# Hybrid decoder block: engines in program order from the first unit on, attention prepared in short steps

## Chip, cores and metric

One core of a Trainium2 chip runs the kernel. The time is device microseconds from launch to the end, the median of several runs. The engines that matter are TensorE (PE), VectorE (DVE), ScalarE (ACT), GpSimd (POOL) and SyncE (SP), which issues the DMAs of the weights.

## What is computed

512 tokens of width 1024 go through one layer: one input projection, two causal mixers (a spatial gating unit and gated linear attention), a gated sum, an output projection, and a feed-forward block, each of the last two followed by a LayerNorm.

```python
p   = x @ W_in + b_in    # u | v | q | k | v_gla | r | a_low | g_A | g_B
y_a = gelu(u) * (W_s @ layer_norm(gelu(v)) + b_s)          # 128-position chunks, 8 groups, causal
log_f = log_sigmoid(a_low @ w_gate2 + b_gate) / 16         # per key channel
# gated linear attention, 4 heads: cum = cumsum(log_f) within a chunk
scores[t, s] = sum_d q[t, d] * k[s, d] * exp(cum[t, d] - cum[s, d])   # s <= t
o   = scores @ v + (q * exp(cum)) @ state
state = exp(total) * state + (k * exp(total - cum)).T @ v
y_b = rms_norm(o) * gla_norm_g * silu(r)
m   = sigmoid(g_A) * y_a + sigmoid(g_B) * y_b
h   = layer_norm(alpha * x + m @ W_out)
out = layer_norm(alpha * h + relu(h @ W_1)**2 @ W_2)
```

## The kernel before

Every fp32 product is made of three fp32r products: an operand is split into a high part (`xh`, `wh`) and the rest (`xl`, `wl`), and `passes` (L194) yields high x high, high x low, low x high. Weights come in chunks of 128x1024: SP loads `raw` (three buffers, L114), ScalarE casts it to `wh` (L92), VectorE subtracts for `wl` (L93). Seven chunks of `wh`, `wl` are kept (`W_BUFS`); `split_to(n)` writes the load, the cast and the subtraction of all chunks up to n at the place in the program where it is called.

The matrix work is cut into units of 24 matmuls of 512 columns, each into one of the four `ps_m` PSUM buffers. The units are counted in slots: slots 0 to 7 are V (two column halves by four token tiles, `row_unit`, L197), 8 to 15 U (`col_job`, L605), 16 to 19 queries and keys of the second pair of heads, 20 to 27 the values VG, 28 to 35 the branch gate GA, 36 to 51 r and g_B, 52 to 59 the output projection. The feed-forward block follows, whose second product is made by seven products of quarter blocks (`seven_products`), the sums of these (`together`, L905) and a last stage `f` (L984) with LN 2 behind it, token tile by token tile. Ahead of slot 0 stand a warm-up of PE on ones (`wu`, L241), q and k of the first pair (`first`, L265) and the low-rank gate input (`pa`, L317).

Attention of a pair of heads is prepared between the units: `at(n, f)` puts a step into slot n and `pump`, called behind each unit, runs what is planned there. The steps of a pair are `gates` (log-sigmoid as Abs, Exp, Ln and a running sum `cum`), three levels of block distance (32, 8, 2), each with `level_diff` (differences of `cum` for key factors `kt` and query factors `qt`), `level_prep` (exponentials, times k and q) and `level_score` for two heads (products `sc`, copied under masks into `AT`), two diagonal scores `sd`, `inter` (the factors `QI`, `kd` between chunks), and `kd_turn` (transposes `pt`, L390). `chunk_out` makes a chunk's output and state. The query differences run on POOL, three instructions for a level (L413).

What sets the order: PE runs in program order from the start. Instructions of VectorE, ScalarE and POOL are ordered by the tile scheduler up to L803, where `manual_schedule` for all engines begins; behind it they too stand as written. The pools around the change: `ps_s` has one buffer (`sc`, `sd`), `ps_a` two (`pz`, `pt`, `pm`, `po`), the tag "kt" one buffer that `ab`, `kd`, `kt` and the diagonal's `dr` share, the tag "qt" two.

Of the kernel before, what the change touches and what calls it, by code (L numbers as in the profile page):

```python
# [8 lines left out]
F32 = mybir.dt.float32  # L9
F32R = mybir.dt.float32r  # L10
# [5 lines left out]
P = 128  # L16
# [24 lines left out]
WARM = (128,) * 7 + (64,) * 5  # L41
QT_BUFS = 2
DIFF_K = "vector"
DIFF_Q = "gpsimd"
MUL_K = "vector"
MUL_Q = "vector"
# [3 lines left out]
def hybrid_block(  # L50
# [131 lines left out]
    plan, slot = {}, [0]  # L182

    def at(n, *fs):
        plan.setdefault(n, []).extend(fs)

    def pump():
        for f in plan.pop(slot[0], []):
            f()
        slot[0] += 1  # L190
# [6 lines left out]
    def row_unit(ah, al, consume):  # L197
# [3 lines left out]
        for ti, t in enumerate(range(NT)):  # L201
            ps = ps_m.tile([P, 512], F32, name=f"ps_{u0}_{t}", tag="ps")
            tsl = slice(t * P, (t + 1) * P)
            for k in range(KT):
                split_to(u0 + max(k // 2 + 1, (W_BUFS if ti < NT - 1 else W_BUFS + k // 2)))
# [6 lines left out]
            pump()  # L212
        split_to(u0 + 4 + W_BUFS)
# [26 lines left out]
    for n in WARM:  # L240
        nc.tensor.matmul(wu[:, :n], ones, ones[:, :n], start=True, stop=True)  # L241
# [108 lines left out]
    def gates(pr):  # L350
        hp = pr.hp
        lf = gt.tile([P, 2, T], F32, name=f"lf{hp}", tag="lf")
        cum = gt.tile([P, 2, T], F32, name=f"cum{hp}", tag="cum")
        ab = gt.tile([P, 2, T], F32, name=f"ab{hp}", tag="kt")
        for j in range(2):
            h = 2 * hp + j
            pz = ps_a.tile([P, 512], F32, name=f"pz{h}", tag="aux")
            nc.tensor.matmul(pz, w2s[:, h * DK : (h + 1) * DK], a_sb, start=True, stop=True)
            bg = col("g2", h)
            nc.scalar.activation(ab[:, j, :], pz, AF.Abs, bias=bg)  # L360
            nc.vector.tensor_scalar(lf[:, j, :], pz, bg, 0.0, op0=ALU.add, op1=ALU.min)
        nc.scalar.activation(ab, ab, AF.Exp, scale=-1.0)
        nc.scalar.activation(ab, ab, AF.Ln, bias=1.0)
        nc.vector.tensor_tensor(lf, lf, ab, op=ALU.subtract)
# [6 lines left out]
        pr.lf, pr.cum = lf, cum  # L371

    def inter(pr):

        hp = pr.hp
        nc.scalar.activation(pr.QI, pr.cum, AF.Exp, scale=1.0 / TEMP)
        nc.vector.tensor_mul(pr.QI, pr.QI, pr.q)
        cv = pr.cum.rearrange("p j (c s) -> p (j c) s", s=P)
        tot = cv[:, :, P - 1 : P]
        nc.scalar.activation(pr.et, tot.rearrange("p c o -> p (c o)"), AF.Exp, scale=1.0 / TEMP)  # L380
        kd = gt.tile([P, 2 * NCH, P], F32, name=f"kd{hp}", tag="kt")
        nc.vector.tensor_tensor(kd, tot.broadcast_to([P, 2 * NCH, P]), cv, op=ALU.subtract)
# [13 lines left out]
    def level_diff(pr, lv):  # L396

        hp, h = pr.hp, LEVELS[lv]
        kt = gt.tile([P, 2 * T], F32, name=f"kt{hp}_{lv}", tag="kt")
        qt = gt.tile([P, 2 * NCH, 192], F32, name=f"qt{hp}_{lv}", tag="qt", bufs=QT_BUFS)  # L400
        nb, na = 2 * T // h, 2 * T // (4 * h)
        cb = flat(pr.cum).rearrange("p (b s) -> p b s", s=h)
        getattr(nc, DIFF_K).tensor_tensor(
            kt.rearrange("p (b s) -> p b s", s=h),
            cb[:, :, h - 1 : h].broadcast_to([P, nb, h]),
            cb,
            op=ALU.subtract,
        )
        c4 = flat(pr.cum).rearrange("p (a i s) -> p a i s", i=4, s=h)
        qv = qt.rearrange("p c n -> p (c n)").rearrange("p (a i s) -> p a i s", i=6, s=h)  # L410
# [8 lines left out]
        pr.kt, pr.qt = kt, qt  # L419

    def level_prep(pr, lv):
        h = LEVELS[lv]
        kt, qflat = pr.kt, pr.qt.rearrange("p c n -> p (c n)")
        nc.scalar.activation(kt, kt, AF.Exp, scale=1.0 / TEMP)
        nc.scalar.activation(qflat, qflat, AF.Exp, scale=1.0 / TEMP)
        getattr(nc, MUL_K).tensor_tensor(kt, kt, flat(pr.k), op=ALU.mult)
        q4 = flat(pr.q).rearrange("p (a i s) -> p a i s", i=4, s=h)
        qv = qflat.rearrange("p (a i s) -> p a i s", i=6, s=h)
        for d, s0 in STEPS:
            n = 4 - d  # L430
            getattr(nc, MUL_Q).tensor_tensor(
                qv[:, :, s0 : s0 + n, :], qv[:, :, s0 : s0 + n, :], q4[:, :, d:4, :], op=ALU.mult
            )

    def diag_prep(pr, j):

        hp = pr.hp
        two = gt.tile([P, 1536], F32R, name=f"dt{hp}_{j}", tag="qt", bufs=QT_BUFS)
        raw = gt.tile([P, 768], F32, name=f"dr{hp}_{j}", tag="kt")
        par = lambda a, o: a[:, j, :].rearrange("p (m o) -> p m o", o=2)[:, :, o]  # L440
        nc.vector.tensor_mul(raw[:, 0:512], pr.q[:, j, :], pr.k[:, j, :])
        pair = raw[:, 512:768]
        nc.scalar.activation(pair, par(pr.lf, 1), AF.Exp, scale=1.0 / TEMP)
        nc.vector.tensor_mul(pair, pair, par(pr.q, 1))
        nc.vector.tensor_mul(pair, pair, par(pr.k, 0))
        split(two[:, 0:768], two[:, 768:1536], raw)
        pr.two = two

    def diag_score(pr, j):
        sc = ps_s.tile([P, 1024], F32, name=f"sd{pr.hp}_{j}", tag="sc")  # L450
        for c0, c1 in ((0, 512), (512, 768)):
            for i in range(2):
                nc.tensor.matmul(
                    sc[:, c0:c1], ones_r, pr.two[:, 768 * i + c0 : 768 * i + c1], start=(i == 0), stop=(i == 1)
                )
        at_ = pr.AT[:, j]
        nc.vector.copy_predicated(
            at_,
            masks[:, 3, 64:192].bitcast(U32).unsqueeze(1).broadcast_to([P, NCH, P]),
            sc[:, 0:512].rearrange("p (c s) -> p c s", s=P),  # L460
        )
        nc.vector.copy_predicated(
            at_.rearrange("p c (m o) -> p c m o", o=2)[:, :, :, 1],
# [668 lines left out]
```

## Time and profile before

| | us |
|---|---|
| median of 3 runs (lowest, highest) | 764.57 (763.75, 764.64) |
| profiled execution | 764.65 |
| its span | 762.9 |
| PE busy | 750.0 |
| VectorE, ScalarE, POOL busy | 489.4, 356.3, 68.1 |

The span is what the trace covers; 1.75 us of the profiled execution lie around it. A busy time counts every instant at which an instruction of the engine ran. PE's matmuls overlap their forerunners, so an interval of 100% can still be a slow one, which the granted clock tells. A wait in the trace is the idle time of an engine ahead of an instruction, put down to the instruction that released it.

### The profile page before, as it was taken

The page shows a single profiled execution, that of the slowest core. Times are in us where ns is not written, and L with a number is a line of the kernel's source. Part 1 is how long each engine was busy: PE and PEld are TensorE (multiplying, and loading weights), DVE is VectorE, ACT ScalarE, POOL GpSimd, SP SyncE. Part 2 cuts the span into 40 slices and gives each one's busy share as a digit, 9 for nine tenths or more (in the row PEclk, how much of TensorE's full clock was granted, in tenths as well). Part 3 has the DMA queues.
Part 4 walks back from the last instruction along what each step waited for, and adds up shares of the span by engine and source line. Part 5 has one row for each costly group of instructions (what it writes and reads, how often), then busy time and mean ns, then how long its engine had stood idle before and what let it go on. Part 6 is the DMA issues. An engine that isn't in the chain of part 4 may idle for free.

```text
span 762.9 us, 8863 instructions
## 1 busy us (share of the span) xinstructions
PE 750.0 (98%) x3504; PEld 628.3 (82%) x3504; DVE 489.4 (64%) x587; ACT 356.3 (47%) x457; POOL 68.1 (9%) x86
## 2 busy tenths in 40 slices
PE   9998999999999999999999999999999999999996
PEld 8887888878888888888888988888888888888785
DVE  7369767668766542454548535774678667778975
ACT  7376864354146444444322444554554544445300
POOL 1015400013302212000001000000000000000011
PEclk9999999999999999999999999999999999999999
DMA  8523332110341232323231423444244433434111
GB/s 338 201 97 104 104 131 82 61 53 26 111 138 56 78 129 82 113 90 104 89 125 63 153 83 99 136 148 142 73 148 139 138 109 113 164 112 165 56 56 55
DMA packets 25465, 85.15 MB, mean 112 GB/s; under 512 B 3088, under 2 KB 3344, under 8 KB 25424
## 3 DMA queue, kind: packets, MB, share of 16 engines
q1 hardware_dynamic: 25280, 84.33, 32.7%
q8 instruction: 27, 0.44, 0.2%
q10 hardware_dynamic: 144, 0.26, 0.1%
q14 instruction: 14, 0.11, 0.0%
HBM read 82.48 MB, written 2.10 MB: 111 GB/s over the span
## 4 chain that ended last, share of the span: by engine, by line
PE 88%; DVE 5%; ACT 3%; issue 2%; POOL 1%; DVEq 0%; POOLq 0%
PE f L602 23%; PE m L898 14%; PE ps L208 12%; PE gb L602 6%; PE r L602 6%; PE u L602 6%; PE f L984 5%; PE ga L602 4%; PE first L265 3%; PE qk L602 2%; PE sc L472 2%; DVE wl L93 1%; POOL qt L413 1%; PE po L498 1%; PE po L500 1%
## 5 line engine op out<-in xcount | busy, mean ns | idle before, releaser
L93 DVE TENSOR_TENSOR wl<-raw,wh 128x1024 fp32r<-128x1024 f32 x141 | 175.0, 1251 | 137.2 <-ACT wh L92 130.6
L92 ACT CAST wh<-raw 128x1024 fp32r<-128x1024 f32 x141 | 145.3, 1045 | 122.7 <-PE ps L208 27.5
L602 PE MATMUL f<-xh,wh 128*128 128x512 f32 (+1 forms) x288 | 105.4, 366 | 0.0
L602 PE MATMUL f<-xl,wh 128*128 128x512 f32 (+1 forms) x288 | 105.2, 365 | 0.0
L602 PE MATMUL f<-xh,wl 128*128 128x512 f32 (+1 forms) x288 | 105.2, 365 | 0.0
L898 PE MATMUL m<-wh,oh 128*128 128x512 f32 x168 | 65.4, 389 | 0.0
L898 PE MATMUL m<-wl,oh 128*128 128x512 f32 x168 | 65.4, 389 | 0.0
L898 PE MATMUL m<-wh,ol 128*128 128x512 f32 x168 | 65.4, 389 | 0.0
L602 PEld LDWEIGHTS f<-xh,wl 128*128 128x128 f32 x288 | 54.3, 189 | 8.8
L602 PEld LDWEIGHTS f<-xl,wh 128*128 128x128 f32 x288 | 54.3, 189 | 8.7
L602 PEld LDWEIGHTS f<-xh,wh 128*128 128x128 f32 x288 | 54.3, 189 | 8.6
L208 PE MATMUL ps<-wh,xh 128*128 128x512 f32 x128 | 51.3, 401 | 0.0
L208 PE MATMUL ps<-wl,xh 128*128 128x512 f32 x128 | 50.1, 391 | 0.0
L208 PE MATMUL ps<-wh,xl 128*128 128x512 f32 x128 | 50.1, 391 | 0.0
L827 ACT ACTIVATE F<-f 128x512 f32<-128x512 f32 (+1 forms) x28 | 15.0, 537 | 72.4 <-PE f L602 72.4
L127 DVE TENSOR_TENSOR raw<-raw,raw 128x1024 f32<-128x1024 f32 x30 | 36.7, 1222 | 8.4 <-DMA raw<-in_w_all 8.4
L413 POOL TENSOR_TENSOR qt<-cum 128x768 f32<-128x768 f32 (+2 forms) x18 | 31.4, 1774 | 115.8 <-DVE cum L368 102.9
L898 PEld LDWEIGHTS m<-wl,oh 128*128 128x128 f32 x168 | 31.6, 188 | 6.6
L898 PEld LDWEIGHTS m<-wh,ol 128*128 128x128 f32 x168 | 31.5, 188 | 6.6
L898 PEld LDWEIGHTS m<-wh,oh 128*128 128x128 f32 x168 | 31.5, 188 | 6.5
L993 POOL TENSOR_TENSOR rs_l<-rs_l,nhalf 128x1 f32<-128x1 f32 x4 | 4.0, 988 | 328.6 <-DVE rs_l L992 328.6
L92 ACT CAST oh<-d 128x1024 fp32r<-128x1024 f32 x15 | 15.8, 1050 | 36.4 <-DVE d L824 36.4
(231 smaller groups left out, 1528.5 us busy)
## 6 DMA issues: line engine op xcount, KB each, us to landing
raw<-in_w_all SPq DMA_DIRECT2D x136, 512.0 KB, 3.3
bufB<-in_head SPq DMA_DIRECT2D x4, 512.0 KB, 7.9
xr<-in_x SPq DMA_DIRECT2D x8, 256.0 KB, 3.7
out<-bufA SPq DMA_DIRECT2D x8, 256.0 KB, 2.0
bufA<-in_head SPq DMA_DIRECT2D x3, 512.0 KB, 5.3
brow<-in_b_in SPq DMA_DIRECT2D x4, 256.0 KB, 5.9
g<-in_ln_g SPq DMA_DIRECT2D x2, 512.0 KB, 4.4
b<-in_ln_b SPq DMA_DIRECT2D x2, 512.0 KB, 4.3
```

What stands on the lines that cost most here:

```text
L92: nc.scalar.copy(hi, src)
L93: nc.vector.tensor_tensor(lo, src, hi.bitcast(F32), op=ALU.subtract)
L127: nc.vector.tensor_tensor(raw, raw, other[0], op=ALU.add if STREAM[i][0] == "sum" else ALU.subtract)
L208: nc.tensor.matmul(ps, s_, m_, start=(k == 0 and i == 0), stop=(k == KT - 1 and i == 2))
L265: nc.tensor.matmul(first[e], s_, m_[:, k, :], start=(k == 0 and i == 0), stop=(k == KT - 1 and i == 2))
L413: getattr(nc, DIFF_Q).tensor_tensor(qv[:, :, s0 : s0 + n, :], c4[:, :, d:4, :], c4[:, :, 0:n, h - 1 : h].broadcast_to([P, na, n, h]), op=A ...
L472: nc.tensor.matmul(sc[:, c, 0:192], pr.kt[:, jc * P : (jc + 1) * P], pr.qt[:, jc, :], start=True, stop=True)
L498: nc.tensor.matmul(po, pr.AT[:, j, c, :], vs, start=True, stop=(c == 0))
L602: nc.tensor.matmul(ps, s_, m_, start=(k == 0 and i == 0), stop=(k == KT - 1 and i == 2))
L827: nc.scalar.activation(dst, ps, AF.Relu)
L898: nc.tensor.matmul(ps, s_, m_, start=(k == 0 and i == 0), stop=(k == 3 and i == 2))
L984: nc.tensor.matmul(ps, s_, m_, start=(f == 0 and i == 0), stop=(f == 7 and i == 2))
```

## The change

The `manual_schedule` of VectorE, ScalarE and POOL (PE had it) now begins behind `low_rank`, ahead of the V units, so all four engines run in the written order from slot 0 on. To write that order, the slots get phases: MID in the middle of a `row_unit`, MM behind the unit's matmuls, MAIN, and LATE behind the unit's chunk splits. The attention steps are cut up over these and lie at other slots:

| step | pair 0 before | after | pair 1 before | after |
|---|---|---|---|---|
| gates | 1 | 0 MID, 1 | 18 | 17, 18 |
| level 0: diff, prep, scores | 3, 3, 5, 6 | 4, 5, 6, 7 | 20, 21, 22, 23 | 21, 23, 24, 25 |
| level 1 | 7, 7, 8, 10 | 7, 8, 9, 10 | 23, 24, 25, 26 | 25, 27, 28, 29 |
| level 2 | 11, 11, 12, 13 | 10, 11, 12, 13 | 26, 26, 28, 29 | 29, 30, 31, 32 |
| diagonal scores | 14, 16 | 15, 16 | 31, 32 | 34, 35 |
| inter | 16 | 2, 3 | 32 | 19, 20 |
| kd_turn (both heads) | 17, 18 | 4 | 33, 34 | 21 |
| mixing of 8 groups | 14 to 21 | 10 to 17 | | |
| chunk_out | 29 to 32 | 28, 31, 32, 33 | 35 to 38 | 36 to 39 |

The query factors of block distance 1 are an exponential of one difference; those of distance 2 and 3 are products of it with the factors of whole blocks between (`whole`, copied by ScalarE). VectorE makes that one difference; the exponential covers 768 elements instead of 1536. `gates_a` puts both heads' products `pz` into one `ps_s` tile. The warm-up is nine matmuls of 128 columns instead of seven of 128 and five of 64. `rstd_of` adds on VectorE. `together` works on one token tile: ahead of the last stage only quarter 7 of tile 0 is summed, the other sums stand behind the pieces of tiles 0 and 1, and `bn_stats` ahead of them.

```diff
-WARM = (128,) * 7 + (64,) * 5
+WARM = 9
...
-            nc.gpsimd.tensor_scalar(dst, src, EPS, None, op0=ALU.add)
+            nc.vector.tensor_scalar(dst, src, EPS, None, op0=ALU.add)
...
             for k in range(KT):
+                if k == KT // 2:
+                    pump(MID)
...
-            pump()
-        split_to(u0 + 4 + W_BUFS)
+            pump(MM, MAIN)
+            if ti == NT - 1:
+                split_to(u0 + 4 + W_BUFS)
+            pump(LATE)
...
+    def gates_a(pr):
+        lf = gt.tile([P, 2, T], F32, name=f"lf{pr.hp}", tag="lf")
+        ab = gt.tile([P, 2, T], F32, name=f"ab{pr.hp}", tag="kt")
+        both = ps_s.tile([P, 2, T], F32, name=f"pz{pr.hp}", tag="sc")
+        heads = [(j, 2 * pr.hp + j) for j in range(2)]
+        for j, h in heads:
+            nc.tensor.matmul(both[:, j, :], w2s[:, h * DK : (h + 1) * DK], a_sb, start=True, stop=True)
+        for j, h in heads:
+            nc.scalar.activation(ab[:, j, :], both[:, j, :], AF.Abs, bias=col("g2", h))
+            nc.vector.tensor_scalar(lf[:, j, :], both[:, j, :], col("g2", h), 0.0, op0=ALU.add, op1=ALU.min)
         nc.scalar.activation(ab, ab, AF.Exp, scale=-1.0)
         nc.scalar.activation(ab, ab, AF.Ln, bias=1.0)
...
+    ctx.enter_context(
+        tc.manual_schedule(
+            engines={getattr(mybir.EngineType, e) for e in ("PE", "DVE", "Activation", "Pool")}
+        )
+    )
...
-        for d, s0 in STEPS:
-            n = 4 - d
-            getattr(nc, DIFF_Q).tensor_tensor(
-                qv[:, :, s0 : s0 + n, :],
-                c4[:, :, d:4, :],
-                c4[:, :, 0:n, h - 1 : h].broadcast_to([P, na, n, h]),
-                op=ALU.subtract,
-            )
...
+        nc.vector.tensor_mul(qv[:, :, 0:3, :], qv[:, :, 0:3, :], q4[:, :, 1:4, :])
+        for o, i0, n in ((3, 1, 2), (5, 4, 1)):
+            nc.vector.tensor_mul(
+                qv[:, :, o : o + n, :],
+                qv[:, :, i0 : i0 + n, :],
+                pr.whole[:, :, 0:n].unsqueeze(3).broadcast_to([P, na, n, h]),
             )
...
+        at(between[0], lambda: gates_b(pr))
+        at(between[1], lambda: inter_a(pr))
+        at(between[1], lambda: inter_e(pr), phase=LATE)
+        at(between[2], lambda: inter_b(pr))
+        kd_turn(between[3], pr)
...
+    at(0, lambda: gates_a(pr0), phase=MID)
+    plan_pair(pr0, (1, 2, 3, 4), ((4, 5, 6, 7), (7, 8, 9, 10), (10, 11, 12, 13)), 13)
...
-            together(7, ((1, 4),))
+            together(7, 0, ((1, 4),))
         if ORDER[n] == 1:
-            together(6, ((1, 3),))
-            together(7, ((1, 1),))
+            together(7, 0, ((1, 1),))
...
-    together(7, ((-1, 5),))
-    together(3, ((1, 5),), (0, 1))
+    together(7, 0, ((-1, 5),))
+    later = {
+        (0, 0): [(6, 0, ((1, 3),)), (3, 0, ((1, 5),), (0, 1))],
+        (0, 1): [(7, 1, ((1, 4), (1, 1), (-1, 5))), (6, 1, ((1, 3),)), (3, 1, ((1, 5),), (0, 1))],
+        (1, 0): [(4, t, ((1, 2),), (1, 0)) for t in range(2)],
+        (1, 1): [(6, t, ((1, 1), (-1, 2))) for t in range(2)],
+    }
...
-            if t == 0:
-                together(*(((4, ((1, 2),), (1, 0))), (6, ((1, 1), (-1, 2))))[pi])
             nc.vector.bn_stats(st2[t][:, pi, :], z[:, sl])
+            for part in later.get((t, pi), ()):
+                together(*part)
```

How the change moves instructions is shown at three places. The first is ScalarE in the V stage, from the cast of chunk 10 on (`bufB<-vt0_n` is the gelu of token tile n, `ab0` the gates of pair 0). Before:

```order
L92 CAST wh10_385<-raw10_372 128x1024
L360 ACTIVATE ab0_450<-pz0_451,cols_sb_101 128x512
L581 ACTIVATE bufB_92<-vt0_1_444 128x512
L360 ACTIVATE ab0_450<-pz1_455,cols_sb_101 128x512
L362 ACT_TABLE_LOAD
L362 ACTIVATE ab0_450<-ab0_450 128x1024
L363 ACT_TABLE_LOAD
L363 ACTIVATE ab0_450<-ab0_450 128x1024
L92 CAST wh11_506<-raw11_374 128x1024
```

After, up to the exponential for QI:

```order
L88 CAST wh10_384<-raw10_369 128x1024
L363 ACTIVATE ab0_403<-pz0_404,cols_sb_101 128x512 x2
L365 ACTIVATE ab0_403<-ab0_403 128x1024
L366 ACT_TABLE_LOAD
L366 ACTIVATE ab0_403<-ab0_403 128x1024
L659 ACT_TABLE_LOAD
L659 ACTIVATE bufB_92<-vt0_0_425 128x512
L659 ACTIVATE bufB_92<-vt0_1_453 128x512
L659 ACTIVATE bufB_92<-vt0_2_492 128x512
L391 ACT_TABLE_LOAD
L391 ACTIVATE QI0_313<-cum0_456 128x1024
```

The gates follow the cast of chunk 10 at once, three gelus stand together behind them, and the exponentials between chunks (`QI`, `kd`, `et`) come ahead of the casts of chunks 11 to 13.

The second place is VectorE in the same stretch, from the subtraction that ends the gates (`vt0_n` takes a unit's result, `sgst` are LayerNorm statistics). Before:

```order
L364 TENSOR_TENSOR lf0_448<-lf0_448,ab0_450 128x1024
L579 TENSOR_TENSOR vt0_2_495<-ps_4_2_470,brow_382 128x512
L368 SCALAR_TENSOR_TENSOR cum0_449<-ones_97,lf0_448 128x128 x8
L93 TENSOR_TENSOR wl11_507<-raw11_374,wh11_506 128x1024
L403 TENSOR_TENSOR kt0_0_546<-cum0_449 128x1024
L582 BN_STATS sgst2_380<-bufB_92 128x6
L93 TENSOR_TENSOR wl12_519<-raw12_376,wh12_518 128x1024
L93 TENSOR_TENSOR wl13_531<-raw13_389,wh13_530 128x1024
L579 TENSOR_TENSOR vt0_3_542<-ps_4_3_499,brow_382 128x512
L426 TENSOR_TENSOR kt0_0_546<-kt0_0_546,k0_313 128x1024
```

After:

```order
L372 TENSOR_TENSOR lf0_402<-lf0_402,ab0_403 128x1024
L376 SCALAR_TENSOR_TENSOR cum0_456<-ones_97,lf0_402 128x128 x8
L661 BN_STATS sgst0_377<-bufB_92 128x6
L657 TENSOR_TENSOR vt0_2_492<-ps_4_2_467,brow_381 128x512
L386 TENSOR_TENSOR kd0_495<-cum0_456 128x1024
L661 BN_STATS sgst1_378<-bufB_92 128x6
L89 TENSOR_TENSOR wl11_509<-raw11_371,wh11_508 128x1024
L89 TENSOR_TENSOR wl12_521<-raw12_373,wh12_520 128x1024
L89 TENSOR_TENSOR wl13_533<-raw13_388,wh13_532 128x1024
L657 TENSOR_TENSOR vt0_3_544<-ps_4_3_501,brow_381 128x512
L396 TENSOR_TENSOR QI0_313<-QI0_313,q0_309 128x1024
L397 TENSOR_TENSOR kd0_495<-kd0_495,k0_310 128x1024
```

The chunk subtractions wl11 to wl13 stand between the difference `kd` and the products for QI and `kd`; behind these, at slot 4, PE transposes `kd`. The level's `kt`, `qt` come later.

The third place is VectorE ahead of the last stage, from the last addition of product 1 on (`Fs`, `xl` are operands of that stage, `bufB` and `acc` the sums of quarters). Before:

```order
L875 TENSOR_TENSOR acc1_3168<-acc1_3168,m2_1_1_5250 128x512
L908 TENSOR_TENSOR bufB_92<-bufB_92 128x2x512
L908 TENSOR_TENSOR bufB_92<-bufB_92,acc1_3168 128x2x512
L93 TENSOR_TENSOR Fs_5278<-Flast_4767,Fs_5278 128x512 x4
L93 TENSOR_TENSOR wl142_5315<-raw142_5228,wh142_5314 128x1024
L93 TENSOR_TENSOR xl_90<-Flast_4767,xh_89 128x512 x4
L875 TENSOR_TENSOR acc5_3170<-acc5_3170,m2_5_0_5328 128x512
L93 TENSOR_TENSOR xl_90<-raw143_5261,xh_89 128x1024
L93 TENSOR_TENSOR wl144_5352<-raw144_5273,wh144_5351 128x1024
```

After:

```order
L958 TENSOR_TENSOR acc1_3165<-acc1_3165,m2_1_1_5247 128x512
L992 TENSOR_TENSOR bufB_92<-bufB_92,acc1_3165 128x512
L89 TENSOR_TENSOR Fs_5274<-Flast_4764,Fs_5274 128x512 x4
L89 TENSOR_TENSOR wl142_5311<-raw142_5225,wh142_5310 128x1024
L89 TENSOR_TENSOR xl_90<-Flast_4764,xh_89 128x512 x4
L958 TENSOR_TENSOR acc5_3167<-acc5_3167,m2_5_0_5324 128x512
L89 TENSOR_TENSOR xl_90<-raw143_5258,xh_89 128x1024
L89 TENSOR_TENSOR wl144_5348<-raw144_5270,wh144_5347 128x1024
L89 TENSOR_TENSOR wl145_5358<-raw145_5314,wh145_5357 128x1024
```

One sum of half the width stands ahead of the operands in the place of two; between the subtractions of the operands nothing has moved.

## Rows read from the trace of the kernel before

**Rows 1.** The page: busy time of each engine, share of the span, instructions.
```profile
PE 750.0 (98%) x3504; PEld 628.3 (82%) x3504; DVE 489.4 (64%) x587; ACT 356.3 (47%) x457; POOL 68.1 (9%) x86
```

**Rows 2.** What PE waited for: us in total, times, longest.
```profile
PE sc L472 <- DVE qt L431: 2.1, 1, 2.1
PE pz L358 <- DVE mx L649: 1.3, 1, 1.3
...
PE f L984 <- DVE xl L93: 0.5, 1, 0.5
PE sc L472 <- DVE AT L484: 0.3, 1, 0.3
PE f L984 <- DVE wl L93: 0.3, 2, 0.2
PE po L498 <- ACT bufB L516: 0.3, 1, 0.3
```

**Rows 3.** Chain of waits, 28 to 110 us: start, us, what.
```profile
49.41 1.23 DVE lf L364
...
51.15 2.62 DVE cum L368 x8
...
66.96 2.61 PE sc L472 x8
69.57 6.07 PE ps L208 x24
75.64 1.30 PE sc L472 x8
76.94 5.45 PE ps L208 x24
```

**Rows 4.** Windows: us, busy of five engines (instructions), PEclk, DMA share, GB/s.
```profile
67.30:70.60 3.30, 3.30 (x11) 3.06 (x10) 2.65 (x5) 3.12 (x3) 0.44 (x2) 0.50 0.15 27
158.20:162.00 3.80, 3.80 (x18) 3.17 (x17) 1.60 (x3) 3.56 (x4) 0.00 (x0) 1.00 0.40 142
```

**Rows 5.** Timeline of PE at 157 us: start, us, engine, line, operation, tiles.
```profile
156.06 0.50 PE L358 MATMUL pz<-a_sb,w2s 128*128 128x512 f32 x1
157.85 0.51 PE L358 MATMUL pz<-a_sb,w2s 128*128 128x512 f32 x1 [1.29 <-DVE mx L649]
```

**Rows 6.** Timeline of POOL in the V stage.
```profile
53.85 12.08 POOL L413 TENSOR_TENSOR qt<-cum 128x768 f32<-128x768 f32 x6 [29.40 <-DVE cum L368]
```

**Rows 7.** Timelines of ScalarE and VectorE, V stage; landing times of weight loads there.
```profile
43.95 0.68 ACT L360 ACTIVATE ab<-pz,cols_sb 128x512 f32<-128x512 f32 x1
44.65 1.28 ACT L362 ACT_TABLE_LOAD   x1
...
33.39 2.36 DVE L93 TENSOR_TENSOR wl<-raw,wh 128x1024 fp32r<-128x1024 f32 x2 [0.19 <-ACT wh L92]
...
43.56 0.75 DVE L361 TENSOR_SCALAR lf<-pz,cols_sb 128x512 f32<-128x512 f32 x1 [0.26 <-ACT ab L360]
...
DMA to landing us min/median/max: 3.1/3.3/4.3
```

**Rows 8.** Timeline of all engines at the start.
```profile
1.07 5.14 PE L241 MATMUL wu<-ones 128*128 128x128 f32 x24 [1.07 <-POOL bal L284]
...
4.29 0.62 ACT L255 CAST xh<-bufA 128x512 fp32r<-128x512 f32 x1 [1.58 <-DMA bufA<-in_head]
...
6.02 1.17 PE L265 MATMUL first<-xh,wh 128*128 128x512 f32 x4
```

**Rows 9.** Timelines of VectorE, ScalarE and PE around the final stage's first matmuls.
```profile
705.55 1.22 DVE L908 TENSOR_TENSOR bufB<-bufB,acc 128x1024 f32<-128x1024 f32 x1
...
713.75 1.05 ACT L92 CAST wh<-raw 128x1024 fp32r<-128x1024 f32 x1 [2.58 <-DMA raw<-in_w_all]
...
713.62 0.39 PE L984 MATMUL f<-xh 128*128 128x512 f32 x1
...
717.36 0.39 PE L984 MATMUL f<-wh,Fs 128*128 128x512 f32 x1
```

More of the change, by code (lines that the diff above doesn't have):

```diff
@@ L239, in hybrid_block @@
     wu = ps_a.tile([P, 512], F32, name="wu", tag="aux")
-    for n in WARM:
-        nc.tensor.matmul(wu[:, :n], ones, ones[:, :n], start=True, stop=True)
+    for i in range(WARM):
+        nc.tensor.matmul(wu[:, :P], ones, ones, start=True, stop=True)
     for i in range(4):
@@ L348, in pair_new, with gates_b @@
         return pr
[L350 to L361, printed above, removed]
+    def gates_a(pr):
[8 more added lines that the diff above has]
+            nc.vector.tensor_scalar(lf[:, j, :], both[:, j, :], col("g2", h), 0.0, op0=ALU.add, op1=ALU.min)
         nc.scalar.activation(ab, ab, AF.Exp, scale=-1.0)
         nc.scalar.activation(ab, ab, AF.Ln, bias=1.0)
-        nc.vector.tensor_tensor(lf, lf, ab, op=ALU.subtract)
+        pr.lf, pr.ab = lf, ab
+    def gates_b(pr):
+        lf = pr.lf
+        cum = gt.tile([P, 2, T], F32, name=f"cum{pr.hp}", tag="cum")
+        nc.vector.tensor_tensor(lf, lf, pr.ab, op=ALU.subtract)
         for j in range(2):
@@ L435, in diag_prep @@
[L435 to L447, printed above, removed]
@@ L629, in hybrid_block, with mix_bias, take @@
         row_unit(xh, xl, v_take(half, bias_row(C_V + half * 512)))
-    def mix_bias():
-        for i in range(2):
-            pb = ps_a.tile([P, 4, P], F32, name=f"pb{i}", tag="aux")
-            nc.tensor.matmul(pb, ones, wst[:, 4 * i : 4 * i + 4, :], start=True, stop=True)
+    def mix_bias(n):
+        def take(i, pb):
             for g in range(4 * i, 4 * i + 4):
@@ L659, in hybrid_block, with products, mix, take @@
-    for g in range(KT):
-        at(S_QK - 2 + g, lambda g=g: mix(g))
+        def products():
+            for i in range(2):
+                pb = ps_a.tile([P, 4, P], F32, name=f"pb{i}", tag="aux")
+                nc.tensor.matmul(pb, ones, wst[:, 4 * i : 4 * i + 4, :], start=True, stop=True)
+                at(n, lambda i=i, pb=pb: take(i, pb))
+        at(n, products, phase=MM)
+    def mix(n, g):
+        gs = slice(g * P, (g + 1) * P)
+        def products():
+            pm = ps_a.tile([P, NCH, P], F32, name=f"pm{g}", tag="aux")
+            for c in range(NCH):
+                nc.tensor.matmul(pm[:, c, :], bufB[:, c, gs], wst[:, g, :], start=True, stop=True)
+            at(n, lambda: take(pm))
+        def take(pm):
+            tm = temp(f"mx{g}")
+            nc.vector.scalar_tensor_tensor(
+                tm.rearrange("p (c s) -> p c s", s=P),
+                pm,
+                col("sgg", g),
+                mixb[:, gs].unsqueeze(1).broadcast_to([P, NCH, P]),
+                op0=ALU.mult,
+                op1=ALU.add,
+            )
+            nc.vector.tensor_mul(AT_[:, g, :], AT_[:, g, :], tm)
+        at(n, products, phase=MM)
```

356 lines of the change are left out of this document (194 added, 162 removed).

## Prediction

> **What bounds the kernel now.** I read the busy table first: PE works in 750.0 us of a span of 762.9 [rows 1]. Such a kernel gets shorter only where PE stands still, or runs slowly after it stood still; work taken from POOL, ScalarE or VectorE is worth nothing by itself. So the second view is the table of what PE waited for [rows 2]. Its rows are the whole budget: 2.1 us for VectorE's query factors `qt`, 1.3 for `mx`, 0.3 for `AT`, 0.3 for `bufB`, and at the end 0.5 for `xl` and 0.3 for `wl`.
>
> The third view is the chain of work around the longest of these, the first score product of pair 0 in the V stage [rows 3]. It came late because its forerunners did: the gates' `lf` at 49.41, the running sums `cum` until 53.77, then the POOL differences, six of them from 53.85 on for 12.08 us [rows 6], the exponentials and VectorE's products. PE's price is more than the 2.1 us of idling [rows 2]. The eight score matmuls behind it took 2.61 us where the next eight took 1.30, and the unit behind them 6.07 where the next took 5.45 [rows 3]. In that stretch the granted clock was 0.50, the lower of its two levels (1.2 instead of 2.4 GHz), right after PE had stood still [rows 4]. So this place costs 2.1 + 1.31 + 0.62 = 4.03 us. The 1.29 us of idling at 157 us [rows 2, 5] cost no clock: behind it the granted clock was 1.00 [rows 4].
>
> **Warm-up.** Twelve warm-up matmuls become nine, 24 passes become 18. The 24 take from 1.07 to the first real matmul at 6.02, 0.206 each; 18 end at 4.78 [rows 8]. The cast of x that the first real matmul needs ends at 4.29 + 0.62 = 4.91 [rows 8], so that matmul comes at most about 1.0 us earlier. If the clock rises when it did, that work runs partly at half speed, worth half; a gain of 0.45 to 0.95 is plausible, nothing the lower bound. I take **-0.65**.
>
> **Attention's preparation, pair 0.** The gates move from slot 1 to the middle of unit 0, so `cum` and all behind it come earlier, and the score product leaves slot 5 for slot 6. POOL's differences, 12.08 us for two levels [rows 6], are replaced by one VectorE difference per level (about 1 us by the 1.22 us of a 1024-wide pass [rows 9]) and products that replace products. The level's path loses some 4 us and gets a unit (5.45 us) more; by my ledger about 1.5 us of slack remains at the score product. The 4.03 us go: **-4.03**.
>
> What is late next? The transposes of `kd` (`pt`), which move from slot 17 to slot 4. All engines now run in program order, so I add up ScalarE's and VectorE's queues from unit 0 on, with the rows' prices: 1.05 us a 1024-wide pass of ScalarE, cast or exponential [rows 9], 1.28 a table load, 0.68 a 512-wide pass there, 1.22 a 1024-wide pass of VectorE, 0.75 a 512-wide one, 2.62 the eight scans [rows 3, 7, 9].
> The cast of wh10 stands ahead of the gates' `Abs` on ScalarE. Its buffer is freed by wl7, at about 34.0 (before, wl7 was the first of the two passes from 33.39 [rows 7], and 0.65 goes off), and the load takes 3.1 us [rows 7]: cast done at 38.1. wl10 on VectorE stands ahead of `lf` in the same way and ends at 39.3. `lf` and `Abs` of the two heads then alternate (both read the same PSUM tile), and the second `Abs` ends at 40.8. Exponential 41.9, table 43.2, logarithm 44.3, subtraction 45.5, scans 48.2, a `bn_stats` and the third token tile's add 49.4, difference `kd` 50.6. ScalarE has loaded the gelu table meanwhile, waits for that token tile, does its gelu (50.1), loads the exp table (51.4), then the exponentials QI 52.4, `kd` 53.5, `et` 53.7, and the casts wh11 to wh13 until 56.7. VectorE has wl11 to wl13 ahead of the products: 58.3, the fourth token tile's add 58.9, QI 60.0, `kd` **61.2**.
> PE meanwhile: unit 0 from 30.9, five units of 5.45 and 0.5 for the gate products: unit 4 ends at 58.7. So PE waits 61.2 - 58.7 = about **+2.4** for `pt`. The ends are 1.4 (the ledger anchored at the end of unit 2 instead) and 3.0. Since 2.1 us cost the clock and 1.29 didn't, I let the clock fall here, at the same price, 1.31 + 0.62: **+1.9**.
>
> The Trainium skill ("ScalarE: Activation LUTs", section "What ACT_TABLE_LOAD costs") puts a switch of tables at 1.283 us of load and 1.38 us of drain. This trace agrees with the load (1.28) but shows no drain ahead of it: the load at 44.65 starts 0.02 us behind the end of the activation before it, 43.95 + 0.68 [rows 7]. By the page two loads of the path above, the logarithm's and that for QI, would each cost 1.4 us more, the wait would be 5.2 and the time 2.8 us above my forecast; the row decides.
>
> **Pair 1 and the mixing.** Both `pz` products of pair 1 go into one tile of `ps_s`, back to back, instead of into two `ps_a` tiles of which the second waited for `mx`. In the timeline the second `pz` starts 1.79 us behind the first [rows 5]; a 512-wide matmul steps by 5.45 / 24 = 0.23 [rows 3]. The gain is 1.79 - 0.23: **-1.56**. The mixing products, four units earlier, have their operands (token tiles normalised by slot 9). The wait for `AT` (0.3) and that for `bufB` (0.3, where a chunk's next product stood right behind the scaling of the one before) lie at products which now have a unit between them: **-0.6**. Against that stand the new tight places, the second diagonal score at slot 35 and the scores at slots 24 and 28, where my ledger leaves 0.5 us or lacks 0.5: **+0.2**.
>
> The smaller edits I cost at nothing. rstd's add moves from POOL to VectorE, one column each, next to idle time on both. The plain-fp32 groups of PE number 34 instead of 40, and no row charges PE for a change of type. Four table loads fewer on ScalarE (33 for 37) are off PE's path except where counted.
>
> **Last sums.** Ahead of the final stage's operand splits VectorE has two 1024-wide sums, the row at 705.55 and one like it before, 1.22 us each [rows 9]; one 512-wide remains (0.75). VectorE reaches the splits 1.7 us earlier. In before, PE's first nine matmuls with late operands took from 713.62 to 717.36, 3.74 us, where nine steps of 0.227 are 2.04 [rows 9], a loss of 1.70 (the three waits of [rows 2] and the smaller delays between). With the `xl` pass 1.7 us earlier only its last part stays tight: **-1.6**, bounds 1.0 and 1.7, and nothing if ScalarE's casts turn out to be the late ones. The postponed sums go behind token tiles 0 and 1, and VectorE has all of tiles 1 and 2, four pieces of 5.45 us, to catch up in; the tail behind PE's end is the same code.
>
> **Sum** against the profiled execution's own 764.65 (the median of the runs is 764.57): -0.65 - 4.03 + 2.4 + 1.9 - 1.56 - 0.6 + 0.2 - 1.6 = -3.94, so 760.7, and **760.6** as a median.
>
> **Rivals.**
> *B, the wait for `pt` comes but the clock stays up*, as behind the 1.29 us: 760.6 - 1.9 = **758.7**. For it: my wait may be as short as 1.4.
> *C, no wait for `pt`*: the load of raw10 lands sooner, or gelu and `kd` overlap more than I let them: 758.7 - 2.4 = **756.3**. Against it: both queues are in order, and the path of 30 us has only durations from rows in it.
> *D, slower.* In before the scheduler let `kt`, `qt` and the masks pass a chunk's cast whose load hadn't landed or whose buffer PE still held. In order, they stand behind it. At slots 24 and 28, in the VG unit, three casts and three subtractions stand ahead of pair 1's level products. If these end 2.7 us later than I count, my 0.5 us of slack becomes a wait of 2.1 us at each, and at the price of the V stage (2.1 + 1.9) twice 4.0 is added: **768.6**. For it: a cast can wait that long for its load, the last one of before waited 2.58 us [rows 9]. Against: 2.7 us is most of a load's 3.1 [rows 7], and the load is issued as soon as a buffer is free.
> *E, the change doesn't do all that it says*: ScalarE's last cast, not VectorE, sets the final stage (+1.6), and the diagonal score at slot 35 waits 0.5: **762.7**.
>
> **Chances.** Forecast 0.45, B 0.24, C 0.11, E 0.12, D 0.08. Range: from C, 756.3, up to just above E, 763.4; what lies outside is D and a part of C. What a measurement of this kernel can tell from no change is about 0.2%, 1.5 us: faster means below 763.0, slower above 766.1. Forecast, B, C and most of E are faster; the rest of E and a milder D are the same: 0.82, 0.10, 0.08.
>
> **What would show it.** In the trace after: the first real matmul near 5.1; no wait at the first `sc`; a wait of PE for `kd` at `pt` near 58.7 of 1.4 to 3.0 us, and a clock of 0.50 behind it; the two `pz` 0.23 us apart; the final stage's operand waits below 0.2 us together. I'd be wrong if PE waits at `sc` in slots 7 to 13 or 24 to 31, if PE's idle time is spread over many short waits behind casts, or if `pt` waits above 3 us.

## The result, and the profile after

The changed kernel takes 759.7 us (median of 6 runs, 758.79 to 760.61); the kernel before, run beside it, 764.52. The ratio is 0.9935, with an interval of 0.9921 to 0.995. The profiled execution took 760.61, its span is 758.9. The six runs fall into two groups, three at 758.8 to 759.0 and three at 760.4 to 760.6; what parts them is shown at experiment 2.

The table of what PE waited for answers to [rows 2]; this is all of it:

```profile
PE pt L403 <- issue: 2.5, 1, 2.5
PE wu L246 <- POOL bal L289: 1.1, 1, 1.1
PE sd L488 <- DVE dt L479: 0.2, 1, 0.2
```

Every wait of [rows 2] is gone. A new one of 2.5 us has come, at the transposes of `kd`, and a short one of 0.2 at a diagonal score; the 1.1 us of the warm-up is the start's. (For the transposes the table names no releaser. The transposes read `kd`, and the VectorE rows below show that its product ended 0.09 us before they began.) The page's busy row answers to [rows 1]: POOL's work is less than half, PE's busy time 1.9 us less.

```profile
PE 748.1 (99%) x3498; PEld 627.9 (83%) x3498; DVE 491.1 (65%) x611; ACT 348.2 (46%) x459; POOL 29.9 (4%) x60
```

In the timeline of PE around that wait (start, us, engine, line, operation, tiles) the columns to look at are the starts:

```profile
58.80 0.39 PE L211 MATMUL ps<-wh,xl 128*128 128x512 f32 x1
61.68 1.94 PE L403 MATMUL pt<-ident,kd 128*128 128x128 f32 x8 [2.49 <-issue]
63.27 0.77 PE L211 MATMUL ps<-wh,xh 128*128 128x512 f32 x1
63.85 0.63 PE L211 MATMUL ps<-wl,xh 128*128 128x512 f32 x1
64.27 0.54 PE L211 MATMUL ps<-wh,xl 128*128 128x512 f32 x1
64.65 0.40 PE L211 MATMUL ps<-wh,xh 128*128 128x512 f32 x1
```

Eight transposes took 1.94 us where others take 1.04, and the unit behind them began with steps of 0.58 and 0.42 instead of 0.23. The windows over the wait and behind it (us, busy of five engines, PEclk) show why, as [rows 4] did before:

```profile
58.00:61.60 3.60, 1.19 (x6) 0.65 (x4) 3.60 (x5) 1.96 (x3) 0.00 (x0) 0.94 0.95 287
61.70:64.60 2.90, 2.90 (x11) 2.70 (x12) 2.90 (x4) 0.64 (x2) 0.00 (x0) 0.51 0.64 254
```

ScalarE's timeline ahead of the wait begins with the wait for the load of chunk 10, as the ledger had it, and ends with the three casts:

```profile
37.78 1.05 ACT L88 CAST wh<-raw 128x1024 fp32r<-128x1024 f32 x1 [2.74 <-DMA raw<-in_w_all]
...
54.16 2.94 ACT L88 CAST wh<-raw 128x1024 fp32r<-128x1024 f32 x3
```

VectorE's:

```profile
55.22 3.50 DVE L89 TENSOR_TENSOR wl<-raw,wh 128x1024 fp32r<-128x1024 f32 x3 [3.31 <-ACT wh L88]
58.64 0.68 DVE L657 TENSOR_TENSOR vt<-ps,brow 128x512 f32<-128x512 f32 x1
59.24 1.21 DVE L396 TENSOR_TENSOR QI<-QI,q 128x1024 f32<-128x1024 f32 x1
60.37 1.22 DVE L397 TENSOR_TENSOR kd<-kd,k 128x1024 f32<-128x1024 f32 x1
```

VectorE was idle for 3.31 us, then subtracted three chunks, and only then came to the product that PE was about to need. It ended at 61.59; the ledger had said 61.2. PE's unit 4 ended later too, at 59.19 (58.80 + 0.39) instead of 58.7, so the two errors nearly cancel in the wait.

At the end, the stretch from the start of the last product matmul `m` to that of PE's last matmul is 755.64 - 710.00 = 45.64 us before and 751.60 - 707.63 = 43.97 after. VectorE's row ahead of the operands is one of half width:

```profile
702.05 0.68 DVE L992 TENSOR_TENSOR bufB<-bufB,acc 128x512 f32<-128x512 f32 x1
702.65 2.49 DVE L89 TENSOR_TENSOR Fs<-Flast,Fs 128x512 fp32r<-128x512 f32 x4
```

### The profile page after: what moved, and what is told of

Read it like the earlier page. It is cut to its first block, busy times and chain, and to the rows that moved or that the text cites. A ratio compares the mean times of both kernels' runs of the same rounds, so it can differ in the third digit from the quotient of the medians.

```text
span 758.9 us, 8804 instructions
## 1 busy us (share of the span) xinstructions
PE 748.1 (99%) x3498; PEld 627.9 (83%) x3498; DVE 491.1 (65%) x611; ACT 348.2 (46%) x459; POOL 29.9 (4%) x60
## 4 chain that ended last, share of the span: by engine, by line
PE 96%; DVE 1%; issue 1%; DMA 0%; ACT 0%; POOL 0%; DVEq 0%; ACTq 0%; POOLq 0%
PE f L686 22%; PE ps L211 17%; PE m L981 15%; PE f L1072 6%; PE r L686 6%; PE gb L686 6%; PE ga L686 6%; PE u L686 6%; PE first L270 3%; PE qk L686 3%; PE sc L514 2%; PE pm L739 1%; PE po L548 1%; PE po L552 1%; PE po L550 1%
## 5 line engine op out<-in xcount | busy, mean ns | idle before, releaser
L89 DVE TENSOR_TENSOR wl<-raw,wh 128x1024 fp32r<-128x1024 f32 x141 | 170.9, 1221 | 100.0 <-ACT wh L88 98.6
L89 DVE TENSOR_TENSOR ol<-d,oh 128x1024 fp32r<-128x1024 f32 x15 | 18.4, 1226 | 16.7 <-ACT oh L88 16.7
L211 PEld LDWEIGHTS ps<-wh,xl 128*128 128x128 f32 x128 | 24.2, 189 | 5.1
```

Of the source, the lines that this page charges most:

```text
L89: nc.vector.tensor_tensor(lo, src, hi.bitcast(F32), op=ALU.subtract)
L211: nc.tensor.matmul(ps, s_, m_, start=(k == 0 and i == 0), stop=(k == KT - 1 and i == 2))
```

## Experiments

Unless another base is named, the edits are to the changed kernel. Times are medians.

**1. The factors between chunks ahead of the chunk subtractions.**

```diff
-        at(between[2], lambda: inter_b(pr))
+        at(*((between[2],) if pr.hp else (between[1],)), lambda: inter_b(pr), phase=MAIN if pr.hp else LATE)
```

> The changed kernel with one step moved: pair 0's products for QI and kd stand right behind their exponentials at slot 2, ahead of the subtractions wl11 to wl13 on VectorE. Theory: the in-order subtractions ahead of kd made TensorE wait 2.5 us at pt, and the half clock behind it cost another 1.6 us; with kd done near 55.6 and pt due at 59.2 both go, so 760.5 - 4.1 = 756.4, in all runs alike (the 1.6 us between the changed kernel's two groups of runs is this clock). Rival 1: the two groups come from the start (the warm-up), then they stay, 756.4 and 758.0. Rival 2: the wait only moves, to wl11 in unit 4 (due at 57.3, now done near 56.8) or to the first score product, then 758 to 760.5.

756.49 us, 4 runs from 756.19 to 757.0. One group, at the number expected. VectorE's timeline shows the order turned round:

```profile
53.06 1.23 DVE L396 TENSOR_TENSOR QI<-QI,q 128x1024 f32<-128x1024 f32 x1 [1.32 <-ACT QI L391]
54.20 1.22 DVE L397 TENSOR_TENSOR kd<-kd,k 128x1024 f32<-128x1024 f32 x1
55.34 3.49 DVE L89 TENSOR_TENSOR wl<-raw,wh 128x1024 fp32r<-128x1024 f32 x3
```

and PE's the transposes at once behind unit 4, at 0.108 us each:

```profile
58.66 0.39 PE L211 MATMUL ps<-wh,xl 128*128 128x512 f32 x1
58.88 1.04 PE L403 MATMUL pt<-ident,kd 128*128 128x128 f32 x8
59.68 0.48 PE L211 MATMUL ps<-wh,xh 128*128 128x512 f32 x1
```

So the wait and its clock cost 758.9 - 754.8 = 4.1 us of the span where both occur.

**2. The changed kernel again.** No edit.

> The changed kernel itself once more, for its two groups of runs (spans of 757.1 and 758.8). Theory: in the lower group TensorE waits for kd just as long but its clock does not fall behind the wait; a profile from that group shows pt and the unit behind it at their usual steps (0.107 and 0.227 us) and a span near 757.2. Rival: the lower group has a faster start (the first real products at full speed from 5.2 us on), pt being the same in both.

759.82 us: three runs at 758.79 to 758.98, three at 760.66 to 761.18, the same groups. The profile was of the upper one (span 759.0), so the lower group has no trace. In its timeline the transposes still ran at full speed:

```profile
61.45 1.06 PE L403 MATMUL pt<-ident,kd 128*128 128x128 f32 x8 [2.57 <-issue]
```

The window behind them shows the clock falling later than in the first trace:

```profile
62.60:65.90 3.30, 3.30 (x9) 2.62 (x8) 3.30 (x6) 2.17 (x3) 0.00 (x0) 0.50 0.65 218
```

The mean granted clock on record for each run settles what parts the groups. In the fourteen traces of this document a fall in the middle of the kernel goes with a mean of 0.993 to 0.996; the traces without one have 0.997 or more. The six upper runs of the two measurements have 0.995 or 0.996, the six lower ones 0.997 or 0.998. So in the lower group the clock did not fall, which is the theory. That PE waited just as long there follows from the time alone, and the second trace speaks against the rival: its first real products ran at full speed, and still the run is an upper one.

**3. The last sums alone**, put into the kernel before (the diff's part on `together` and `later`).

> The kernel before with the last sums alone taken from the change (by token tile, the postponed ones behind the pieces of tiles 0 and 1, bn_stats ahead of them). Theory: VectorE reaches the operands of the last stage 1.7 us earlier and the waits for xl and wl go, 764.5 - 1.6 = 762.9. Rival: ScalarE's last cast, which waited 2.58 us for its load, sets the stage, then 764.0 to 764.5. A second rival: the postponed sums delay the LayerNorm tail, then above 764.5.

763.81 us (12 runs, 762.14 to 765.06), ratio 0.999, interval 0.9978 to 1.0002: by the medians undecided, since the runs lie in two groups, six at 762.1 to 763.1 and six at 764.5 to 765.1. The kernel before, run beside it, has the same two, fourteen runs at 763.9 to 764.7 and three at 766.25 to 766.48; group against group the mean falls by 1.6 and by 1.5 us, as the theory had it. The trace agrees: the final stretch is 753.30 - 709.33 = 43.97 us, 1.67 less than before, and no wait for `xl` or `wl` is left. The rest is in the V stage. The profiled run's table of PE's waits has the first score product as [rows 2] have it, and more waits at later ones:

```profile
PE sc L472 <- DVE qt L431: 2.1, 1, 2.1
...
PE sc L472 <- DVE AT L484: 0.9, 2, 0.6
PE sc L472 <- DVE kt L426: 0.4, 1, 0.4
```

The window behind the first of these waits:

```profile
66.50:69.70 3.20, 3.20 (x16) 2.87 (x17) 2.98 (x5) 2.70 (x3) 0.10 (x1) 1.00 0.02 6
```

The clock stayed up, so the unit behind came at full speed, and the next score products waited instead, 0.75 and 0.53 us more from start to start than their step. The half-speed stretch of [rows 3] had covered these. The upper group has no trace; its mean clock on record is 0.997 to 0.999, so it is not the fall behind this wait that makes it.

**4. The query factors as before**, in program order.

```diff
-        nc.vector.tensor_tensor(pr.qv[:, :, 0:3, :], c4[:, :, 1:4, :], ...)
+        for d, s0 in STEPS:
+            n = 4 - d
+            nc.gpsimd.tensor_tensor(pr.qv[:, :, s0 : s0 + n, :], c4[:, :, d:4, :], ...)
```

(and the exponential of 1536 elements and three products with q, as before)

> The changed kernel with the query factors made as before: three POOL differences for a level, an exponential of 1536 elements, three products with q. Theory: the slots and the in-order queues took away the wait at the first score product, since POOL can start its differences as soon as the running sums are there, so no wait at sc comes back; POOL at work beside VectorE slows wl11 to wl13 (before, two such took 3.94 instead of 2.36 us), which makes the wait at pt longer by up to 1.6, so 760.5 to 762.1. Rival: the products were needed, the first score product is late again, then 763 or above.

760.22 us (5 runs, 760.04 to 760.51). No wait came back at the first score product. Two short ones came at later ones. The table of PE's waits:

```profile
PE pt L403 <- issue: 2.5, 1, 2.5
...
PE sc L512 <- DVE AT L525: 0.3, 1, 0.3
PE sc L512 <- DVE kt L457: 0.3, 1, 0.3
```

The wait at `pt` is as long as in the changed kernel, yet the transposes ran at full speed and the granted clock in the window behind it was 1.00:

```profile
61.30 1.06 PE L403 MATMUL pt<-ident,kd 128*128 128x128 f32 x8 [2.46 <-issue]
```

```profile
61.30:64.50 3.20, 3.20 (x18) 2.79 (x19) 3.20 (x5) 0.92 (x2) 0.00 (x0) 1.00 0.70 237
```

This is the same wait with the clock up, which the second experiment has no trace of. In all five runs the mean clock on record is 0.997 to 0.999, so the runs to compare with are the lower group of the changed kernel (758.8 to 759.0): POOL's factors cost 1.3 us here, and the two short waits, 0.41 and 0.50 us beyond PE's step, are 0.9 of it. POOL was at work from 48.69 for 4.11 us, so it was done when VectorE came to wl11 to wl13; the longer wait that the theory allowed for didn't come.

**5. The gates one slot earlier, in the kernel before.** One number, the first of `plan_pair(pr0, 0, (1, 3, 3, ...))`, from 1 to 0.

> The kernel before with one number changed: pair 0's gates at slot 0 instead of 1, the scheduler ordering VectorE, ScalarE and POOL as before. Theory: the first score product was late because its chain began late, so one unit earlier (5.45 us) is more than the 2.1 us wait; the wait and the half clock behind it (together up to 4.0 us) go, but about 1.3 us come back as waits at the next two score products, which the slow stretch had covered (0.75 and 0.53 us in the run with the sums alone, whose clock did not fall). So 764.2 - 2.7 = 761.5. Rival: the scheduler fills the freed time with other work ahead of the score's factors, the wait stays, 763.8 to 764.5.

768.42 us (6 runs, 767.65 to 769.89; the kernel before beside it 766.33), ratio 1.0038, interval 1.0024 to 1.0053: slower, and neither theory foresaw it. The first score product's wait is down to 0.2 us, and the second level's waits 4.2, with the clock at half behind it:

```profile
PE sc L472 <- DVE kt L426: 4.2, 1, 4.2
```

The chain ahead of it goes through ScalarE's normalisation of a token tile, which stood in line for POOL's small LayerNorm instructions, and these behind POOL's differences:

```profile
75.62 3.50 POOL qt L413 x3
...
79.20 1.09 POOL rs_sg L171
...
80.36 1.61 POOL rs_sg L174
...
83.51 1.98 ACT wh L92 x2
...
85.50 1.28 ACT L424
86.80 1.06 ACT kt L424
...
87.89 1.24 DVE kt L426
```

In the kernel before that normalisation and two casts stand behind the second level's exponential, which began at 84.92; here they stand ahead of it, and it began at 86.80.

**6. Factors first, and the scheduler.** Experiment 1 without the early `manual_schedule`:

```diff
-    ctx.enter_context(
-        tc.manual_schedule(
-            engines={getattr(mybir.EngineType, e) for e in ("PE", "DVE", "Activation", "Pool")}
-        )
-    )
```

> The version with pair 0's factors first, but VectorE, ScalarE and POOL ordered by the scheduler up to the feed-forward block, as before; slots, phases and short steps stay. Theory: the slots and the removal of the POOL work are what counts, the order by the scheduler costs at most a short wait or two: 756.5 to 757.5. Rival: program order is needed; left to the scheduler, work for later slots gets ahead of what TensorE waits for next, and waits at sc or pt of 1 us or more return: 758 or above.

755.44 us (4 runs, 755.19 to 755.6), 1.05 less than in program order; neither theory had it gain. The only entry left among PE's waits is that of the warm-up. The gain sits where program order had left small things. In the changed kernel's trace the second matmul of the diagonal score of slot 35 started 0.70 us behind the first, and the second LayerNorm transposes began 0.33 us behind the matmul before them, where 0.12 is its step. Counted from stage to stage by PE's first matmuls, 0.6 us less are in the GA units and 0.5 in the feed-forward block.

**7. The gate products in two tiles of `ps_a`**, on experiment 1.

```diff
-        both = ps_s.tile([P, 2, T], F32, name=f"pz{pr.hp}", tag="sc")
...
+            both.append(ps_a.tile([P, 512], F32, name=f"pz{h}", tag="aux"))
```

> The version with pair 0's factors first, but the two gate products of a pair in two tiles of the pool of two buffers, as before, instead of in one tile of ps_s. Theory: at slot 17 the second product again waits for VectorE to empty the mixing product's buffer, 1.3 to 1.5 us more: 756.5 + 1.4 = 757.9. Rival: moving the mixing and the gates apart had already removed this wait, 756.5 (pair 0's Abs and lf no longer take turns at one tile there, which puts nothing on TensorE's path).

758.32 us (5 runs, 758.1 to 758.74): 1.8 more than experiment 1. In PE's timeline the wait is back, with a pool of two buffers as before; its last releaser is now VectorE's `lf` of the pair's first product. The last mixing product still stands in this slot: it holds the other buffer from 147.97 on, and VectorE takes it at 152.81, behind both `lf`. So the size is the theory's and the releaser is not:

```profile
148.77 0.48 PE L362 MATMUL pz<-a_sb,w2s 128*128 128x512 f32 x1
150.88 0.51 PE L362 MATMUL pz<-a_sb,w2s 128*128 128x512 f32 x1 [1.62 <-DVE lf L365]
```

**8. The old warm-up**, on experiment 1.

> The version with pair 0's factors first with the old warm-up (24 passes instead of 18). By the prediction's term it is 0.65 us slower, 757.1; by the starts traced so far (the V units begin at 31.54 and 31.07 us with the old warm-up, at 30.97 to 31.32 with the new) it is 0.2 slower, 756.7, and within the scatter. Rival: the real products that run at half speed at the start use up all that the shorter warm-up gives, 756.5.

756.65 us: four runs at 756.24 to 756.85, two at 758.85 and 759.12. The median lies between the two theories and does not part them. The traced start isn't later than with nine matmuls: the V units begin at 30.92 us, in experiment 1 at 31.18.

**9. The change without program order**: the diff of experiment 6, on the changed kernel itself.

> The changed kernel with one part undone: VectorE, ScalarE and POOL are ordered by the scheduler up to the feed-forward block, as before; slots, phases, steps and products stay. In the scheduler's order the products for QI and kd stand ahead of wl11 to wl13 by themselves. Theory: program order is what made TensorE wait at pt (2.5 us and up to 1.6 of half clock) and at the diagonal score and the LayerNorm transposes (about 1.0 together), so 759.8 - 4.1 - 1.0 = 755 to 756, in one group of runs. Rival: the wait at pt belongs to the slots, it stays, 758 to 760.

755.24 us (4 runs, 755.1 to 755.49), ratio 0.9874, interval 0.9855 to 0.9893: with experiments 6 and 12 the fastest version, 4.5 us below the change as made. No wait of PE is left but the start's. The scheduler by itself puts `kd` ahead of the chunk subtractions:

```profile
50.94 1.22 DVE L397 TENSOR_TENSOR kd<-kd,k 128x1024 f32<-128x1024 f32 x1
52.07 1.22 DVE L89 TENSOR_TENSOR wl<-raw,wh 128x1024 fp32r<-128x1024 f32 x1
```

**10. The scheduler with POOL's factors**: experiments 4 and 6 together.

> The version with pair 0's factors first and the scheduler, with the query factors made as before (three POOL differences a level, an exponential of 1536 elements, three products with q). Theory: with the new slots the way the factors are made is off TensorE's path except for two short waits at score products in the U units (0.4 and 0.5 us in the run with POOL's factors in program order), so 755.4 + 0.9 = 756.3. Rival: the scheduler lets the POOL differences and the work they slow on VectorE reach the first score products, as in the kernel before, 758 or above.

758.74 us (6 runs, 758.51 to 759.77), 3.3 more than experiment 6. So the way the factors are made does count, which the theory denied. Here VectorE worked beside POOL, which ran for 10.06 us from 46.45 on, and its two `kd` passes took 2.15 and 2.56 us, those of experiment 9 1.21 and 1.22:

```profile
46.87 2.15 DVE L386 TENSOR_TENSOR kd<-cum 128x1024 f32<-128x1024 f32 x1
...
51.58 2.56 DVE L397 TENSOR_TENSOR kd<-kd,k 128x1024 f32<-128x1024 f32 x1
54.06 3.00 DVE L454 TENSOR_TENSOR qt<-qt,q 128x768 f32<-128x768 f32 x2
```

wl11 came too late for unit 4 (0.8 us), and a score product waited 1.6:

```profile
PE sc L512 <- DVE rs_sg L167: 1.6, 1, 1.6
...
PE ps L211 <- DVE wl L89: 0.8, 1, 0.8
PE sc L512 <- DVE AT L525: 0.3, 1, 0.3
```

**11 and 12. The warm-up once more**, both versions beside each other on experiment 9.

> The scheduled version of the changed kernel with the old warm-up (24 passes). In the run with the old warm-up and in the runs of the kernel before some runs lie 2.2 to 2.6 us above the rest; in the versions with the new warm-up and no wait at pt none does. Theory: the second group belongs to the long warm-up (its end and the first real products meet the clock in another way), so about a third of these runs lie near 757.5 to 758, the others at 755.2, and a profile of the upper group would show half-speed products in the first stage. Rival: the groups belong to the chip and the moment, then this version and the same one with the new warm-up beside it spread alike.

> The scheduled version of the changed kernel once more, beside the one with the old warm-up. Theory: all runs within 755.1 to 755.7, no second group. Rival: it shows the same groups as its neighbour.

Old: 755.74 us, three runs at 755.07 to 755.74, two at 757.4 and 757.88. New: 755.33, four runs at 754.95 to 755.78. With experiments 1, 6, 7 and 9 that is none of 21 runs in an upper group with the new warm-up (where PE doesn't wait at `pt`), and with experiment 8 four of 11 with the old one. The kernel before, which has the old warm-up too, shows 13 such runs among the 39 beside experiments 1 to 10. Every profile with the old warm-up was of a lower group, so where the upper one loses its 2 us stays open. A fall of the clock behind a wait it is not: the four upper runs have a mean clock of 0.997 to 0.999.

## Why the prediction was right, step by step

The forecast was 760.6, with 758.7 if the clock stays up behind the wait at `pt` (rival B). The upper group of runs, 760.4 to 760.6 in the first measurement, is the one, the lower, 758.8 to 759.0, the other; the median lies between. The upper group is traced twice, both times with the clock down; that the lower is the one with it up is seen in the mean clock of its runs (experiment 2), not in a trace of its own. The forecast and rival B came six times each in twelve runs, where the chances given were 0.45 and 0.24; which of the two a run takes the prediction could not say.

The terms:

- *The first score product* (-4.03): no wait is left, the whole term came. That the short steps' slots do it, more than the products, is seen in experiment 4, in program order; in the scheduler's order a wait of 1.6 us at a score product comes back with POOL's factors (experiment 10).
- *The wait at `pt`* (+2.4): 2.49, with `kd` 0.4 us and PE 0.5 us later than in the ledger; that these cancel is luck. *The clock* (+1.9): about 1.5 (the transposes 1.94 instead of 1.04, the three steps behind them 0.6 more). Experiment 1 gives both together as 4.1, against 4.3.
- *`pz`* (-1.56): the wait is gone, and experiment 7, which gives the products their two buffers in `ps_a` again, brings a wait of that size back. The move of the mixing alone would not have removed it, since the last mixing product still stands in that slot.
- *`AT`, `bufB`* (-0.6): gone; counted from start to start beyond PE's step, they were 0.50 and 0.44 us. *The diagonal score* (+0.2): 0.46. A loss of 0.4 us at the LayerNorm transposes and in the stage around them was not foreseen; I had stopped the ledger ahead of it.
- *The last sums* (-1.6): 1.67, alone in experiment 3 as well.
- *The warm-up* (-0.65) was the step that failed as it was put. The first real matmul came at 5.18, as said, but its successors ran at half speed longer: the four of the first group took 1.79 us instead of 1.17 [rows 8]. And the prediction had looked at the cast of x alone. The second group needs VectorE's rest `xl`, which ends at 6.2 to 6.4 us with either warm-up. In the four traces with the new one whose first products ran at full speed or nearly so, PE's weight load waited 0.41 to 0.51 us for it, as the second trace of the changed kernel shows below. The V units begin at 30.84 to 31.64 in nine traces with the new warm-up and at 30.92 to 31.63 in five with the old, 0.2 apart in the mean. What the new one does is another thing: the upper group of runs is missing. In the mean over runs experiments 11 and 12 differ by 1.0 us, experiments 8 and 1 by 0.8.

PE at the start of the changed kernel in its first trace:

```profile
1.07 4.21 PE L246 MATMUL wu<-ones 128*128 128x128 f32 x18 [1.07 <-POOL bal L289]
5.18 1.79 PE L270 MATMUL first<-xh,wh 128*128 128x512 f32 x4
6.81 1.09 PE L270 MATMUL first<-xl,wh 128*128 128x512 f32 x4
```

and the weight load of the second group in its second trace (experiment 2):

```profile
6.35 0.77 PEld L270 LDWEIGHTS first<-xl,wh 128*128 128x128 f32 x4 [0.50 <-DVE xl L262]
```

The sum so came out for the right reasons in its large terms, and with some luck in the small ones. As measured, the terms are -0.2 for the start, -4.0 + 2.5 + 1.5 for the first score product, the wait and its clock, -1.6 for `pz`, -0.9 for `AT` and `bufB`, +0.5 for the diagonal score, +0.4 around the LayerNorm transposes and -1.7 for the last sums: -3.5, where the two profiled executions differ by 4.04. The other 0.5 us is spread over steps too short to assign. What the sum did not ask was what program order is worth. It took the whole change as one thing; experiment 9 shows that one of its parts, the one that the change is named for, costs 4.5 us, and that the others together gain 9.1 (764.38 to 755.24). Rival C, no wait at `pt`, is what a single moved step gives (experiment 1: 756.5, forecast 756.3). Of rival D nothing was seen: PE waited at neither slot 24 nor slot 28 in any trace in program order.

Experiment 5 shows why the one cheap edit that the profile suggests, an earlier start of the late chain, wouldn't have done: the first score product came in time, the scheduler put other work ahead of the second level's exponential, and the next product up the chain became the late one.

## What to carry to other kernels

An engine's queue written out by hand is a promise about every instruction in it: add up, in order, what stands ahead of the step that the bottleneck needs next, with the durations of the trace, loads included. Thirty microseconds ahead such a ledger was 0.4 us off here, and the mend that it suggests (the product ahead of three subtractions that aren't yet due) brought 3.3 us of median. And when a change both moves steps and fixes the order, measure the two apart: here the new slots, the lighter factors, the shared `pz` tile and the last sums were the gain and the fixed order the loss.

## What the runs showed of the hardware

**The clock behind a wait falls or doesn't.** After idling of 2.1 to 2.6 us the granted clock of PE fell to 0.50 in three traces (the kernel before, the changed kernel twice) and stayed at 1.00 in two (experiments 3 and 4), with a wait of the same length and nearly the same start; behind the 4.2 us of experiment 5 it fell as well. In the changed kernel's first trace it had fallen before the wait ended (0.94 over 58.0 to 61.6, and slow transposes), in its second 1.1 us behind the wait's end (62.6). The Trainium skill ("TensorE: Matmul & The Clock Gate", "Part 1: The HAM clock gate (the "warmup" mystery)") has a clock gate that judges PE's activity on a grid that runs free of the program. That would make the outcome a matter of how the wait falls on that grid; no run here sets that phase, so it is argued and not shown. For a forecast it means two times with a gap rather than one. How wide the gap is depends on what stands behind: in the changed kernel 1.6 us or a little more. In the kernel before, seven of the fourteen lower runs beside experiments 1 to 4 have a mean clock of 0.996 (764.2 to 764.7) and seven of 0.997 or 0.998 (763.9 to 764.2), 0.4 us apart in the mean. That fits experiment 3, where later waits took back what the full clock gave.

**At the start the clock's column says nothing yet.** In the changed kernel the first 512-wide products stepped by 0.56, 0.43 and 0.41 us and then by 0.23, in stretches for which the window shows 1.00:

```profile
5.60:6.20 0.60, 0.60 (x3) 0.41 (x3) 0.60 (x2) 0.28 (x1) 0.00 (x0) 1.00 1.07 437
```

The first record of the clock in this trace begins at 6.54 us, where the steps become short, and the column shows a stretch without a record as full. So ahead of it the steps have to be read, not the column.

**VectorE beside POOL.** Passes over 1024 elements with two operands in SBUF took 1.50 to 2.56 us instead of 1.22 while POOL computed differences (experiment 10; one in experiment 4 took 1.57). Passes over 512 elements beside the same differences, with one operand in PSUM or with one operand alone, kept their 0.68. The Trainium skill ("SBUF — State Buffer", section "SBUF: two separate sides") has VectorE, in an operation with two SBUF inputs, and GpSimd take one pair of ports from each other, for a whole instruction. On which passes are slowed the rows agree; that it is for whole instructions they don't show.
